# Turning attention values token-major with VectorE's 32x32 block transposes and stores of 128-byte pieces, in place of TensorE transposes and copies

## The chip, the core and the metric

The kernel runs on one core of a Trainium2 chip. The engines are TensorE (PE in the profile; its weight loads are a row of their own, PEld), VectorE (DVE), ScalarE (ACT), GpSimd (POOL) and SyncE (SP), which only issues DMAs. DMAs are issued here from SP's queue (hardware) and from GpSimd's (software). The metric is the device time of one execution, in microseconds (us), as the median of the runs shown.

## The reference: what is computed

A residual stream of 1024 tokens by 1024 features passes through two layers: a gated short convolution, and an attention over dilated windows. Only the second is touched. Cut to what matters:

```python
h = rms_norm(x, attn_norm)
proj = h @ w_in                       # per dilation group g of 3: q, k, v (1024 columns each); then z
for g, (window, dilation) in enumerate(((128, 1), (512, 4), (2048, 16))):
    q, k = rms_norm(q_g, q_gain[g]), rms_norm(k_g, k_gain[g])
    # query t attends to keys t - dilation*j: the sequence is split into `dilation`
    # residue classes, each evaluated in banded blocks of 128 queries
    logits = q @ k.T * HEAD_DIM ** -0.5 + bias          # 16 heads of 64
    out_g, lse_g = softmax(logits) @ v_g, logsumexp(logits)
o = sum over g of softmax_over_g(lse_g) * out_g
x = x + (o * silu(z)) @ w_out
```

## The kernel before, in words

The program runs in four stages, of which the third is the one that is edited: (1) the convolution's input projections, 0 to some 620 us; (2) its output projection, up to some 862 us; (3) the projections of the attention layer, to some 1622 us, here called the projection stage; (4) the attention itself with its output projection, to the end.

Data lie with features on the 128 partitions and tokens along the free axis. Matrix products are made in float32r: each operand is split into a high part (`ACTIVATE ws<-...`, line 164, on ScalarE) and a low part (`TENSOR_TENSOR ws<-...`, line 165, on VectorE), and three products (lines 301, 303, 304) make one.

In the projection stage two blocks of 128 output columns are taken together, as a *pair*, by seven Strassen-like products of 12 matmuls each. `pairs` (line 598) lists 40 of them: two pairs of kind "qk" (each the q and k of one *unit*, a unit being a head pair `hp` and a dilation group `g`), then one of kind "v" (the values of the same two units), twelve times over, with four pairs of kind "z" between and behind. TensorE takes the products of pair n in the order 1, 2, 4 of the pair before, 6, 5, 3 of the pair before, 7. In the profile a product is known by its right-hand operand: 1 `blke`, 2 `blkf`, 4 `blka`, 6 `xb`, 5 `blkd`, 3 `blkb`, 7 `blkg`. Products 1, 6, 7 and 4 of one pair add up in one PSUM bank `v["x"]`. After 1, 6 and 7 ScalarE copies the bank's state out (`copied`, line 309), and the next product of the bank can begin when that copy is done; after 4, the finished result is taken. VectorE adds these copies to the other bank (`added`, line 313). A result goes to `got`: for "qk" it is squared and summed; for "v" it is multiplied by the tokens' norm factors `R1` into a spare SBUF area (`blkc` in the profile, line 682), on VectorE when it comes from PSUM and on GpSimd otherwise.

Weights are loaded by SP (`wr`, line 159), mixed by GpSimd (`sr`, line 276) and split into eight rotating buffers `ws`. While pair n is multiplied, one split of pair n + 1 follows each product.

The attention needs V token-major: tokens on partitions, the two heads' 128 features along the free axis. `turn(col, q)` does that for half the tokens of one unit: four TensorE transposes against `ident` into one PSUM bank (line 729), one copy to an SBUF tile `f` (VectorE for q = 1, line 732; ScalarE for q = 0, line 734) and one store of 256 KB to the DRAM tile `vd` from GpSimd's queue (line 735). The four turns of a "v" pair n stand behind the products 2, 4, 6 and 5 of pair n + 2. That pair has no `norm`, the work on q and k which stands in the pairs two behind each "qk" pair. In stage (4) `load_v` (line 839) fetches a unit's V with two DMAs of 128 partitions from SP's queue, two steps before the unit's first step.

The order on TensorE is the order of the code in stages (1) to (3) (`manual_schedule`); the other engines' order there is set by a scheduler from its own estimates. In stage (4) all engines keep the order of the code. Each engine works strictly in its order. Completions of DMAs from SP (and from ScalarE, had it any) are counted on eight semaphores, `DMAHW0` to `DMAHW7`, which the framework hands out in turn; a DMA that reuses one waits until the previous DMA on it has landed.

Of the kernel before, what the change touches and what calls it, by code (L numbers as in the profile page):

```python
# [10 lines left out]
F32 = mybir.dt.float32  # L11
F32R = mybir.dt.float32r
I32 = mybir.dt.int32
AF = mybir.ActivationFunctionType
OP = mybir.AluOpType
# [4 lines left out]
P = 128  # L20
D = 1024
S = 1024
KT = D // P
HALF = 512
# [4 lines left out]
HP = H // 2  # L29
G = 3  # L30
# [5 lines left out]
def trunk(ctx: ExitStack, tc: tile.TileContext, a, out):  # L36
    nc = tc.nc
    consts = ctx.enter_context(tc.tile_pool(name="consts", bufs=1))
    dram = ctx.enter_context(tc.tile_pool(name="dram", bufs=1, space=DRAM))
# [32 lines left out]
    ident = const("ident", [P, P])  # L72
# [43 lines left out]
    sk1 = dram.tile([H, P * 385], F32, name="sk1")  # L116
    sk2 = dram.tile([H, P * 257], F32, name="sk2")
    qkd = dram.tile([HP, G, 2, P, S], F32, name="qkd")
    vd = dram.tile([HP, G, 2, P, HALF], F32, name="vd")
    zd = dram.tile([HP, P, S], F32, name="zd")  # L120
    nld = dram.tile([HP, 2, S * 4], F32, name="nld")
    fd = dram.tile([HP, G, 2, S], F32, name="fd")
# [1 line left out]

    def half(hf):
        return slice(hf * HALF, hf * HALF + HALF)

    def blk(t, g, b):
        if g == 0:
            return t[:, b * P:(b + 1) * P]  # L130
        if g == 1:
            return t.rearrange("p (n s c) -> p c n s", n=2, c=4)[:, b // 2, b % 2]
        return t[:, b * P:(b + 1) * P]

    with tc.tile_pool(name="wq", bufs=1) as wq, tc.tile_pool(name="sle", bufs=1) as sle, \
            tc.tile_pool(name="sl", bufs=1) as sl, \
# [370 lines left out]
        with tc.tile_pool(name="ev", bufs=1, side="right", reuse_waits="tile") as ev, tc.tile_pool(name="xb", bufs=1, side="right", reuse_waits="tile") as xb, \  # L507
# [122 lines left out]
            units = [(hp, g) for hp in range(HP) for g in range(G)]  # L630
# [16 lines left out]
            def spare():  # L647
                if not space:
                    space["t"] = block("c").rearrange("p a b c -> p (a b c)").bitcast(F32)
                return space["t"]  # L650
# [6 lines left out]
            def pair(n, w):  # L657
                p = pairs[n]
# [3 lines left out]
                def got(col, hf, t, ps=None):  # L662
                    cs = half(hf)
                    if kind == "qk":
                        if ps is not None:
                            t = copied(ps)
                        u[col, hf] = t
                        if "st" not in u:
                            u["st"] = sm.tile([P, 2, 32], F32, name="st", tag="st")
                        sq = ftile()  # L670
                        nc.scalar.activation(sq, t, AF.Square)  # L671
                        nc.vector.tensor_reduce(out=u["st"][:, col, hf * 16:(hf + 1) * 16],
                                                in_=sq.rearrange("p (c q) -> p c q", q=32), op=OP.add, axis=AX.X,
                                                apply_transpose=True)
                    elif kind == "v":
                        vt = spare()[:, col * S + hf * HALF:col * S + hf * HALF + HALF]
                        eng, t, r = (nc.vector, ps, R1[:, cs]) if ps is not None else (nc.gpsimd, t, R1[:, cs])
                        if units[p[1] + col][1] == 2:
                            vt = spare()[:, col * S:col * S + S].rearrange("p (r x i) -> p i x r", r=4, x=4)
                            vt = vt[:, hf * 32:hf * 32 + 32]  # L680
                            t, r = (y.rearrange("p (i x r) -> p i x r", x=4, r=4) for y in (t, r))
                        eng.tensor_tensor(vt, t, r, op=OP.mult)  # L682
                    else:
                        if ps is not None:
                            t = ftile()
                            nc.vector.tensor_tensor(t, ps, R1[:, cs], op=OP.mult)
                        else:
                            nc.gpsimd.tensor_tensor(t, t, R1[:, cs], op=OP.mult)
                        nc.scalar.activation(t, t, AF.Silu)
                        nc.gpsimd.dma_start(zd[p[1] + col, :, cs], t)  # L690
# [29 lines left out]

                def turn(col, q):
                    hp, g = units[p[1] + col]
                    vt = spare()[:, col * S:col * S + S]
                    if q:
                        pv = cps.tile([P, 4, P], F32, name="pp", tag="pp")
                    else:
                        pv = cst.tile([P, 4, P], F32, name="st", tag="st")
                    for i in range(4):
                        nc.tensor.transpose(pv[:, i], blk(vt, g, 4 * q + i), ident)
                    o = ftile()  # L730
                    if q:
                        nc.vector.tensor_copy(o, pv.rearrange("p a b -> p (a b)"))
                    else:
                        nc.scalar.activation(o, pv.rearrange("p a b -> p (a b)"), AF.Copy)
                    nc.gpsimd.dma_start(vd[hp, g, q], o)

                if kind == "qk":
                    due[n + 2, 0] = [norm]
# [76 lines left out]
    with tc.tile_pool(name="sp", bufs=1, space=PSUM) as sp, tc.tile_pool(name="ptp", bufs=2, space=PSUM) as ptp, \  # L815
# [11 lines left out]
        QK, VS, SZ, y2, part, ml = {}, {}, {}, {}, {}, {}  # L827
# [10 lines left out]

        def load_v(hp, g):
            VS[hp, g] = ap.tile([P, 8, P], F32, name="V", tag="V", bufs=3)  # L840
            for q in range(2):
                nc.sync.dma_start(VS[hp, g][:, 4 * q:4 * q + 4].rearrange("p a b -> p (a b)"), vd[hp, g, q])


        banks = [sp.tile([P, 4, P], F32, name="ps", tag=f"ps{i}") for i in range(3)]
# [337 lines left out]
        for un in units:  # L1183
            st, prefetch = attention(*un)
# [16 lines left out]
        for r in range(3):  # L1201
            k0 = at[2 * r + 2, 0][0] + LD
            k = k0
            for i, (dt, hf) in enumerate(tiles):
                late = k >= len(steps)
                name = "pd"
# [125 lines left out]
```

## Time and profile before

| what | value |
|---|---|
| runs | 1952.8, 1958.64, 1959.34 us; median 1958.64 |
| span of the profiled execution | 1952.1 us |
| its time outside the span | not recorded apart; the span is 0.7 us below the lowest run |
| busy share of PE, PEld, DVE, ACT, POOL | 98%, 79%, 77%, 45%, 44% |
| projection stage | 862 to 1622 us |
| stores of `vd` | 48, 256 KB each |

The profile is taken from one execution. A row of a group gives its line, engine, operation, tiles written and read, and the durations of one instruction as minimum, median and maximum in ns. A row of a timeline gives start, duration, engine, line, operation. A row of the waits gives who waited for whom, us in total, times, the longest. Matmuls overlap, so their durations say less than the distance of their starts.

### The profile page before, as it was taken

The page shows a single profiled execution, that of the slowest core. Times are in us where ns is not written, and L with a number is a line of the kernel's source. Part 1 is how long each engine was busy: PE and PEld are TensorE (multiplying, and loading weights), DVE is VectorE, ACT ScalarE, POOL GpSimd, SP SyncE. Part 2 cuts the span into 40 slices and gives each one's busy share as a digit, 9 for nine tenths or more (in the row PEclk, how much of TensorE's full clock was granted, in tenths as well). Part 3 has the DMA queues.
Part 4 walks back from the last instruction along what each step waited for, and adds up shares of the span by engine and source line. Part 5 has one row for each costly group of instructions (what it writes and reads, how often), then busy time and mean ns, then how long its engine had stood idle before and what let it go on. Part 6 is the DMA issues. An engine that isn't in the chain of part 4 may idle for free.

```text
span 1952.1 us, 30599 instructions
## 1 busy us (share of the span) xinstructions
PE 1906.1 (98%) x10894; PEld 1549.5 (79%) x10894; DVE 1495.5 (77%) x2769; ACT 886.4 (45%) x2031; POOL 850.0 (44%) x775
## 2 busy tenths in 40 slices
PE   8999999999999999999999999999999999889999
PEld 6888888888888888888878888878888886667777
DVE  7866766666665655698898689869888886889996
ACT  6433333333333444453433433444343437877780
POOL 0366666676665211433444443444344442433330
PEclk9999999999999999999999999999999999999999
DMA  6312232323223665432323232232232336887852
GB/s 200 117 58 89 87 94 85 101 72 103 79 84 109 215 208 189 138 103 87 129 87 124 92 111 101 103 108 97 87 129 87 127 110 243 253 278 230 250 149 87
DMA packets 117033, 253.79 MB, mean 130 GB/s; under 512 B 17726, under 2 KB 23070, under 8 KB 116880
## 3 DMA queue, kind: packets, MB, share of 16 engines
q1 hardware_dynamic: 93280, 176.89, 28.0%
q0 software_dynamic: 23600, 74.95, 11.4%
q8 instruction: 85, 1.39, 0.3%
q14 instruction: 68, 0.56, 0.1%
HBM read 192.53 MB, written 67.64 MB: 133 GB/s over the span
## 4 chain that ended last, share of the span: by engine, by line
PE 77%; DVE 11%; issue 4%; DMA 4%; ACT 2%; POOL 1%; SPq 0%; DVEq 0%; POOLq 0%; ACTq 0%
PE pp L301 18%; PE pp L304 18%; PE pp L303 18%; PE pp L552 3%; PE pp L553 3%; PE pp L551 3%; DVE ws L165 2%; DVE blkc L716 2%; PE pt L949 2%; PE po L970 1%; PE pp L374 1%; PE pp L376 1%; PE pp L375 1%; ACT xs L942 1%; DVE ri L67 1%
## 5 line engine op out<-in xcount | busy, mean ns | idle before, releaser
L165 DVE TENSOR_TENSOR ws<-wr,ws 128x512 fp32r<-128x512 f32 x284 | 273.1, 963 | 120.3 <-ACT ws L164 119.2
L164 ACT ACTIVATE ws<-wr 128x512 fp32r<-128x512 f32 x284 | 178.3, 629 | 355.0 <-PE pp L304 232.3
L164 ACT ACTIVATE ws<-sr 128x512 fp32r<-128x512 f32 x272 | 169.9, 629 | 294.1 <-PE pp L304 235.1
L276 POOL TENSOR_TENSOR sr<-wr 128x512 f32<-128x512 f32 x136 | 186.7, 1373 | 260.8 <-DMA wr<-in_conv_w_in 68.1
L165 DVE TENSOR_TENSOR ws<-sr,ws 128x512 fp32r<-128x512 f32 x272 | 226.6, 841 | 77.8 <-ACT ws L164 75.6
L313 DVE TENSOR_TENSOR f<-pp,f 128x512 f32<-128x512 f32 x204 | 139.5, 684 | 87.3 <-PE pp L304 80.6
L942 ACT ACTIVATE xs<-xs,nl 128x256 f32<-128x256 f32 (+2 forms) x384 | 160.4, 423 | 0.0
L309 ACT ACTIVATE f<-pp 128x512 f32<-128x512 f32 x228 | 132.5, 581 | 24.6 <-POOL blkc L682 11.0
L671 ACT ACTIVATE f<-f 128x512 f32<-128x512 f32 x96 | 60.7, 632 | 138.4 <-DVE f L313 100.9
L276 POOL TENSOR_TENSOR sr<-wr,sr 128x512 f32<-128x512 f32 x68 | 88.4, 1301 | 71.3 <-issue 46.8
L301 PE MATMUL pp<-blkg,ws 128*128 128x512 f32 x272 | 107.3, 394 | 4.6 <-ACT f L309 4.6
L936 DVE CUSTOM_DVE_ANT_0 xs<-ps,bt 128x256 f32<-128x256 f32 (+2 forms) x384 | 102.3, 324 | 10.1 <-ACT xs L942 4.2
L301 PE MATMUL pp<-blkf,ws 128*128 128x512 f32 x272 | 108.6, 399 | 0.7 <-ACT f L309 0.7
L301 PE MATMUL pp<-blka,ws 128*128 128x512 f32 x272 | 107.3, 394 | 1.5 <-ACT f L309 1.5
L301 PE MATMUL pp<-blkb,ws 128*128 128x512 f32 x272 | 107.3, 395 | 0.0
L276 POOL TENSOR_TENSOR sr<-sr,wr 128x512 f32<-128x512 f32 x68 | 104.9, 1543 | 4.9
L301 PE MATMUL pp<-blkd,ws 128*128 128x512 f32 x272 | 107.0, 393 | 0.0
L304 PE MATMUL pp<-blkf,ws 128*128 128x512 f32 x272 | 106.3, 391 | 0.0
L304 PE MATMUL pp<-blkd,ws 128*128 128x512 f32 x272 | 106.0, 390 | 0.0
L304 PE MATMUL pp<-blka,ws 128*128 128x512 f32 x272 | 106.0, 390 | 0.0
L304 PE MATMUL pp<-blkb,ws 128*128 128x512 f32 x272 | 106.0, 390 | 0.0
L303 PE MATMUL pp<-blkg,ws 128*128 128x512 f32 x272 | 105.9, 389 | 0.0
(341 smaller groups left out, 5271.7 us busy)
## 6 DMA issues: line engine op xcount, KB each, us to landing
wr<-in_conv_w_in SPq DMA_DIRECT2D x128, 256.0 KB, 3.1
wr<-in_wqk SPq DMA_DIRECT2D x96, 256.0 KB, 3.0
qkd<-blkc POOLq DMA_DIRECT2D x48, 512.0 KB, 3.4
qk<-qkd SPq DMA_DIRECT2D x48, 512.0 KB, 5.2
wr<-in_conv_w_out SPq DMA_DIRECT2D x64, 256.0 KB, 3.2
f<-in_x SPq DMA_DIRECT2D x48, 256.0 KB, 4.4
wr<-in_wv SPq DMA_DIRECT2D x48, 256.0 KB, 3.2
vd<-f POOLq DMA_DIRECT2D x48, 256.0 KB, 2.6
```

The source lines that it names most:

```text
L164: nc.scalar.activation(t[:, 0], src, AF.Copy)
L165: nc.vector.tensor_tensor(t[:, 1], src, t[:, 0].bitcast(F32), op=OP.subtract)
L276: nc.gpsimd.tensor_tensor(t, x, y, op=op)
L301: nc.tensor.matmul(ps, w[:, 0, ws], b[:, k, 0], start=new and k == 0, stop=False, skip_group_check=not new)
L303: nc.tensor.matmul(ps, w[:, 0, ws], b[:, k, 1], start=False, stop=False, skip_group_check=not new)
L304: nc.tensor.matmul(ps, w[:, 1, ws], b[:, k, 0], start=False, stop=end and k == 3, skip_group_check=not new)
L309: nc.scalar.activation(t, ps, AF.Copy)
L313: nc.vector.tensor_tensor(m, ps, m, op=OP.add)
L551: nc.tensor.matmul(ps[dt], w[:, 0, ws], b[:, k, 0], start=(q == k == 0), stop=False)
L671: nc.scalar.activation(sq, t, AF.Square)
L936: nc.vector.tensor_tensor_reduce(out=x, in0=flat[s][:, cols], in1=u["bt"][s][:, bs], op0=OP.add, op1=OP.min, scale=-1.0, scalar=3e38, accu ...
L942: nc.scalar.activation(x, x, AF.Exp, bias=nm, scale=-1.0, accum_out=L)
```

## The change

`turn` no longer uses TensorE or PSUM. The multiplication in `got` writes V into the spare area in an order in which a 32x32 block transpose of VectorE (each block of 32 partitions by 32 elements turned by itself) leaves, on partition 32a + q, tokens q and features 32a to 32a + 31 as runs of 32 floats. Four DMAs from ScalarE's queue store the tile, one for each block of 32 partitions, each as 32 x 16 pieces of 128 bytes, to a `vd` that has another shape. `load_v` fetches it by four DMAs of 32 partitions, 4 KB per partition. For the third dilation group the multiplication is made in two halves.

```diff
-    vd = dram.tile([HP, G, 2, P, HALF], F32, name="vd")
+    vd = dram.tile([HP, G, 32, 32, P], F32, name="vd")
...
                     elif kind == "v":
-                        vt = spare()[:, col * S + hf * HALF:col * S + hf * HALF + HALF]
+                        vt = spare()[:, col * S:col * S + S]
                         eng, t, r = (nc.vector, ps, R1[:, cs]) if ps is not None else (nc.gpsimd, t, R1[:, cs])
-                        if units[p[1] + col][1] == 2:
-                            vt = spare()[:, col * S:col * S + S].rearrange("p (r x i) -> p i x r", r=4, x=4)
-                            vt = vt[:, hf * 32:hf * 32 + 32]
-                            t, r = (y.rearrange("p (i x r) -> p i x r", x=4, r=4) for y in (t, r))
-                        eng.tensor_tensor(vt, t, r, op=OP.mult)
+                        g = units[p[1] + col][1]
+                        if g == 0:
+                            vt = vt.rearrange("p (x n b q) -> p n b x q", x=4, n=2, b=4)[:, hf]
+                            t, r = (y.rearrange("p (b x q) -> p b x q", b=4, x=4) for y in (t, r))
+                        elif g == 1:
+                            vt = vt.rearrange("p (x c n q) -> p n c x q", x=4, c=4, n=2)[:, hf]
+                            t, r = (y.rearrange("p (x q c) -> p c x q", x=4, c=4) for y in (t, r))
+                        if g == 2:
+                            vt = vt.rearrange("p (x n c h q) -> p n h x c q", x=2, n=2, c=4, h=2)[:, hf]
+                            t, r = (y.rearrange("p (q h x c) -> p h x c q", h=2, x=2, c=4) for y in (t, r))
+                            for h in range(2):
+                                eng.tensor_tensor(vt[:, h], t[:, h], r[:, h], op=OP.mult)
+                        else:
+                            eng.tensor_tensor(vt, t, r, op=OP.mult)
...
                 def turn(col, q):
                     hp, g = units[p[1] + col]
-                    vt = spare()[:, col * S:col * S + S]
-                    if q:
-                        pv = cps.tile([P, 4, P], F32, name="pp", tag="pp")
-                    else:
-                        pv = cst.tile([P, 4, P], F32, name="st", tag="st")
-                    for i in range(4):
-                        nc.tensor.transpose(pv[:, i], blk(vt, g, 4 * q + i), ident)
+                    vt = spare()[:, col * S + q * HALF:col * S + q * HALF + HALF]
                     o = ftile()
-                    if q:
-                        nc.vector.tensor_copy(o, pv.rearrange("p a b -> p (a b)"))
-                    else:
-                        nc.scalar.activation(o, pv.rearrange("p a b -> p (a b)"), AF.Copy)
-                    nc.gpsimd.dma_start(vd[hp, g, q], o)
+                    nc.vector.transpose(o.rearrange("p (c q) -> p c q", q=32), vt.rearrange("p (c q) -> p c q", q=32))
+                    to = vd[hp, g].rearrange("q c (a d) -> a q c d", d=32)[:, :, 16 * q:16 * q + 16]
+                    for a in range(4):
+                        nc.scalar.dma_start(to[a], o[32 * a:32 * a + 32].rearrange("q (c d) -> q c d", d=32))
...
         def load_v(hp, g):
             VS[hp, g] = ap.tile([P, 8, P], F32, name="V", tag="V", bufs=3)
-            for q in range(2):
-                nc.sync.dma_start(VS[hp, g][:, 4 * q:4 * q + 4].rearrange("p a b -> p (a b)"), vd[hp, g, q])
+            for x in range(4):
+                nc.sync.dma_start(VS[hp, g][32 * x:32 * x + 32], vd[hp, g, :, 8 * x:8 * x + 8])
```

What it moves is seen in the first pair with `turn`. On TensorE, between products 2 and 4, there stood before:

```order
L304 MATMUL pp<-blkf,ws 128x512
L729 MATMUL st<-ident,blkc 128x128 x4
L301 MATMUL pp<-blka,ws 128x512
L303 MATMUL pp<-blka,ws 128x512
L304 MATMUL pp<-blka,ws 128x512
```

Now the first matmul on `blka` follows the last on `blkf`; so it does at all 48 places.

On ScalarE the same pair ran as follows before (the first row is the square behind a "qk" result, the row of L734 the copy of the first turn):

```order
L671 ACTIVATE f<-f 128x512
L734 ACTIVATE f<-st 128x512
L164 ACTIVATE ws<-wr 128x512
L309 ACTIVATE f<-pp 128x512
L671 ACTIVATE f<-f 128x512
L164 ACTIVATE ws<-sr 128x512
L309 ACTIVATE f<-pp 128x512
L734 ACTIVATE f<-st 128x512
L164 ACTIVATE ws<-sr 128x512 x2
L671 ACTIVATE f<-f 128x512
L164 ACTIVATE ws<-wr 128x512
L309 ACTIVATE f<-pp 128x512
```

and runs as follows now (line numbers of the changed kernel: 157 for 164, 302 for 309, 664 for 671):

```order
L664 ACTIVATE f<-f 128x512
L730 DMA vd<-f 32x16x32 x4
L157 ACTIVATE ws<-wr 128x512
L302 ACTIVATE f<-pp 128x512
L664 ACTIVATE f<-f 128x512
L157 ACTIVATE ws<-sr 128x512
L302 ACTIVATE f<-pp 128x512
L730 DMA vd<-f 32x16x32 x8
L157 ACTIVATE ws<-sr 128x512
L730 DMA vd<-f 32x16x32 x4
L157 ACTIVATE ws<-sr 128x512
L664 ACTIVATE f<-f 128x512
```

Behind the last row follow, as before, one split and the copy of `v["x"]` after product 7. The second and third turn's stores stand together behind the copy after product 6, and the fourth's behind one split more. With what they wait for, the second to the fourth turn's stores read:

```order
L730 DMA vd<-f 32x16x32 [waits DVE_49]
L730 DMA vd<-f 32x16x32
L730 DMA vd<-f 32x16x32 [waits DMAHW4_49]
L730 DMA vd<-f 32x16x32 [waits DMAHW5_49]
L730 DMA vd<-f 32x16x32 [waits DMAHW6_49,DVE_49]
L730 DMA vd<-f 32x16x32 [waits DMAHW7_49]
L730 DMA vd<-f 32x16x32 [waits DMAHW0_49]
L730 DMA vd<-f 32x16x32 [waits DMAHW1_49]
L157 ACTIVATE ws<-sr 128x512 [waits PE_49]
L730 DMA vd<-f 32x16x32 [waits DMAHW2_49,DVE_49]
L730 DMA vd<-f 32x16x32 [waits DMAHW3_49]
L730 DMA vd<-f 32x16x32 [waits DMAHW4_49]
```

`DVE_49` is VectorE's block transpose. Semaphores 4 and 5 were last used by a load of weights, 6, 7, 0 and 1 by the first turn's stores, and those of the fourth turn's stores (2 to 5) by the second turn's.

VectorE's part of the same place, before:

```order
L165 TENSOR_TENSOR ws<-wr,ws 128x512
L672 TENSOR_REDUCE st<-f 128x16
L165 TENSOR_TENSOR ws<-wr,ws 128x512
L732 COPY f<-pp 128x512
L672 TENSOR_REDUCE st<-f 128x16
```

and now:

```order
L158 TENSOR_TENSOR ws<-wr,ws 128x512
L727 STREAM_TRANSPOSE f<-blkc 128x512
L665 TENSOR_REDUCE st<-f 128x16
L158 TENSOR_TENSOR ws<-wr,ws 128x512
L727 STREAM_TRANSPOSE f<-blkc 128x512 x3
L665 TENSOR_REDUCE st<-f 128x16
```

The first block transpose stands one split earlier than the first copy did, and the other three together where it stood.

More of the change, by code (lines that the diff above doesn't have):

```diff
@@ L126, in half @@
         return slice(hf * HALF, hf * HALF + HALF)
[L128 to L133, printed above, removed]
     with tc.tile_pool(name="wq", bufs=1) as wq, tc.tile_pool(name="sle", bufs=1) as sle, \
```

## The prediction

> **What bounds the kernel now.** I read the page first (busy shares, chain), then the busy time by stage, then the stage in which the change lies, in order of time.
>
> ```profile
> PE 1906.1 (98%) x10894; PEld 1549.5 (79%) x10894; DVE 1495.5 (77%) x2769; ACT 886.4 (45%) x2031; POOL 850.0 (44%) x775
> PE 77%; DVE 11%; issue 4%; DMA 4%; ACT 2%; POOL 1%; SPq 0%; DVEq 0%; POOLq 0%; ACTq 0%
> 862.00:1622.00 760.00, 750.40 (x3390) 615.25 (x3389) 632.57 (x944) 298.70 (x520) 323.17 (x300) 1.00 0.31 108
> 1622.00:1800.00 178.00, 160.11 (x2210) 120.52 (x2209) 154.98 (x662) 143.96 (x582) 58.90 (x74) 0.96 0.82 256
> PE pp L301 <- ACT f L309: 6.0, 13, 1.3
> PEld pp L301 <- ACT f L309: 11.9, 14, 1.8
> PE st L694 <- DVE st L672: 2.8, 8, 0.4
> PE st L729 <- POOL blkc L682: 0.8, 1, 0.8
> ACT ws L164 <- PE pp L304: 243.5, 167, 2.7
> ```
>
> The third and fourth rows are stages: length, then busy time of PE, weight loads, DVE, ACT and POOL, granted clock, DMA share, GB/s. The removed transposes lie in the projection stage, 862 to 1622: TensorE is busy 750.4 of 760.0 us at full clock, the DMA engines 31%. The next four rows are TensorE's waits there: for the copies of L309 under 2 us each, for VectorE and GpSimd 3.6 us in all. The last says that ScalarE, with the splits of the weights, waits for TensorE to free their buffers: it is ahead. A microsecond taken from TensorE's row of instructions is therefore worth a microsecond, until another engine makes TensorE wait. What an instruction of that row costs has to be read from starts, since matmuls overlap:
>
> ```profile
> 1165.72 0.39 PE L303 MATMUL pp<-blkd,ws 128*128 128x512 f32 x1
> 1165.95 0.39 PE L304 MATMUL pp<-blkd,ws 128*128 128x512 f32 x1
> 1166.18 0.60 PE L729 MATMUL pp<-ident,blkc 128*128 128x128 f32 x4
> 1166.53 0.48 PE L301 MATMUL pp<-blkb,ws 128*128 128x512 f32 x1
> 1166.85 0.39 PE L303 MATMUL pp<-blkb,ws 128*128 128x512 f32 x1
> ```
>
> Products start every 0.227 us (1165.72 to 1165.95, rounded). From 1165.95 to 1166.85 are 0.90 us for two steps, which alone take 0.453: four transposes cost 0.447 us.
>
> **The change, part by part.**
>
> ```profile
> L729 PE MATMUL st<-ident,blkc x96: 270/272/385, 894.0 to 1609.8; 128*128 128x128 f32 x96
> L729 PE MATMUL pp<-ident,blkc x96: 270/272/286, 897.1 to 1613.0; 128*128 128x128 f32 x96
> L732 DVE COPY f<-pp x24: 676/687/693, 900.0 to 1613.3; 128x512 f32<-128x512 f32 x24
> L734 ACT ACTIVATE f<-st x24: 577/586/594, 897.3 to 1610.2; 128x512 f32<-128x512 f32 x24
> L735 POOL DMA_DIRECT2D vd<-f x48: 540/540/600, 902.4 to 1614.3; - x48
> L704 DVE STREAM_TRANSPOSE f<-ri x96: 667/669/714, 861.0 to 1592.1; 128x512 f32<-128x512 f32 x96
> L682 DVE TENSOR_TENSOR blkc<-pp,sqacc x12: 645/652/1055, 883.0 to 1592.7; 128x512 f32<-128x512 f32 x12
> L682 POOL TENSOR_TENSOR blkc<-f,sqacc x36: 1278/1304/1792, 858.6 to 1600.7; 128x512 f32<-128x512 f32 x36
> ```
>
> 1. TensorE loses 192 transposes, 48 groups of four: 48 x 0.447 = 21.5 us, all on the path.
>
> 2. VectorE loses 24 copies of 0.687 and gets 48 block transposes, which the row of L704 prices at 0.669: 32.1 - 16.5 = +15.6 us over the stage, in which it is busy 632.6 of 760. All of it falls in the 12 pairs that hold `turn`, which have no `norm`. I take 0; what hides it is that pair's idle time on VectorE. ScalarE loses 24 x 0.586 = 14.1 us, GpSimd 48 x 0.54 = 25.9 us of issuing.
>
> 3. The multiplications of V write another order. For the second dilation group the reads become strided (4 instructions on VectorE, 12 on GpSimd); the third already was, and is the maximum of both L682 rows: from 0.652 up to 1.055 and from 1.304 up to 1.792, so 4 x 0.40 + 12 x 0.49 = 7.5 us at most, and 0 at least. For the third group each becomes two halves, a fixed cost more. Only where a copy of L309 waits for a tile that GpSimd still reads does it reach TensorE: I take 2 us.
>
> 4. The stores are the open term. 48 of 256 KB on GpSimd's queue become 192 of 64 KB on ScalarE's, each 512 pieces of 128 bytes. ScalarE issues in order, so whatever an issue costs, and whatever it waits for, delays the copies, squares and weight splits behind it. I call the price of one issue c. No DMA is issued from ScalarE now. The nearest rows:
>
> ```profile
> L879 SPq DMA_DIRECT2D bt<-sk x32: 319/320/1221, 1603.2 to 1854.0; - x32
> L877 SPq DMA_DIRECT2D bt<-sk x32: 444/546/1485, 1623.3 to 1862.6; - x32
> L990 POOL DMA_DIRECT2D nld<-nl x8: 902/908/927, 1638.1 to 1881.1; - x8
> L992 POOL DMA_DIRECT2D nld<-nl x8: 727/732/740, 1646.9 to 1895.4; - x8
> ```
>
> L879 moves 128 pieces of 1 KB on SP's hardware queue in 0.32, L877 64 pieces of 256 bytes in 0.55. GpSimd's queue, whose price grows with the pieces, takes 0.73 for 256 (L992) and 0.91 for 1024 (L990), so some 0.78 for 512. The ends are 0.32 and 0.91. I take 0.55: L877 is nearest in kind (a hardware queue, small pieces, part of the partitions), and L879 against it shows no growth with the count of pieces. What TensorE can bear is read from the first pair with `turn`:
>
> ```profile
> 893.96 0.60 PE L729 MATMUL st<-ident,blkc 128*128 128x128 f32 x4
> 896.65 0.68 DVE L165 TENSOR_TENSOR ws<-wr,ws 128x512 fp32r<-128x512 f32 x1
> 897.77 0.62 ACT L164 ACTIVATE ws<-wr 128x512 fp32r<-128x512 f32 x1
> 898.30 0.59 ACT L309 ACTIVATE f<-pp 128x512 f32<-128x512 f32 x1
> 910.25 0.58 ACT L309 ACTIVATE f<-pp 128x512 f32<-128x512 f32 x1
> 915.22 0.39 PE L301 MATMUL pp<-blka,ws 128*128 128x512 f32 x1
> ```
>
> In the new order VectorE makes the first block transpose behind the split of 896.65, done near 898.0. Then ScalarE issues 4 stores (4c), runs five instructions at one start per 0.53 us (897.77 to 898.30; 2.7 us), issues 8, runs one, issues 4, runs three and then the copy that stood at 910.25 (12c, and 2.7 us for the five). So that copy ends at 898.0 + 5.4 + 16c = 903.4 + 16c. TensorE needs it, since the product on `blka` adds to the bank that it reads: 915.22 before, and 4 x 0.447 earlier once the four groups from 893.96 on are gone, 913.4. The slack is 10.0 - 16c: 1.2 us at c = 0.55, none at c = 0.625; beyond it each of the 12 pairs costs 16c - 10.0. The splits of weights are delayed too, but each takes the one of eight buffers that a product has just left, and is used six products or more later: 6 x 12 x 0.227 = 16 us. At c = 0.55 I take 0.
>
> 5. The program counts hardware DMAs on eight semaphores that SP and ScalarE share; the last four stores of a pair wait until the second four have landed. Issue to issue between these lie 8c + 0.5 = 4.9 us, and 1.2 of slack: landings up to 6.1 us cost nothing.
>
> ```profile
> vd<-f POOLq DMA_DIRECT2D x48, 256.0 KB, 2.6
> nld<-nl POOLq DMA_DIRECT2D x1, 16.0 KB, 2.0
> DMA to landing us min/median/max: 1.8/5.8/10.5
> ```
>
> The second row is the store of L992 at 1895, 256 pieces of 64 bytes with the DMA engines idle: 2.0 us. The third holds all transfers through `nld`, in a stage with the DMA engines 82% busy. The stage of the change has 31%, so I take about 3 us, hidden. [...]
>
> 6. V is loaded by 4 transfers of 32 partitions in place of 2, 48 issues more on SP:
>
> ```profile
> 1627.02 1.89 SPq L842 DMA_DIRECT2D V<-vd  x2
> 1640.04 1.09 PE L970 MATMUL po<-pts,V 128*64 128x128 f32 x16
> SPq L877 <- DMA bt<-sk: 8.7, 4, 3.5
> ```
>
> This load, the tightest that I found, is issued 13 us before its first use, so 2 x 0.4 us of issues more are hidden. SP already waits there for earlier landings (third row), and doubling may stretch that; 0 to 3 us, I take 0.
>
> The sum: 1952.1 - 21.5 + 2 = 1932.6 for the profiled span. That span is 0.7 below the lowest of the three runs and 6.5 below their median, 1958.64; on the median the forecast is 1958.64 - 19.5 = 1939.1.
>
> **The rivals.**
>
> Rival 1, slower: the issue price. If 512 pieces cost ScalarE what GpSimd's rows say, c = 0.78 to 0.91, the `blka` product waits 2.5 to 4.6 us for the copy of L309 in each of 12 pairs, 30 to 55 us: 1969 to 1994. It cancels the gain at 16c - 10.0 = 19.5 / 12, c = 0.73. For it: the pieces are four times any hardware DMA's here, in three dimensions, and L877 is dearer than L879. Against it: L877 moves half the pieces.
>
> Rival 2, slower: the pieces land late. With landings of 10.5 us, the maximum above, 10.5 - 6.1 = 4.4 us by 12 pairs are 53 us: 1992. Against it: the 2.0 us, and idle DMA engines.
>
> Rival 3, no change: VectorE and GpSimd take it back. If all 7.5 us of part 3 and the 15.6 us of part 2 came to TensorE, -21.5 + 23.1 gives 1960. Against it: the 3.6 us in the first fence, and GpSimd is relieved of 25.9.
>
> In between lies c from 0.63 to 0.76, where TensorE gives part or all of it back: 1940 to 1965.
>
> **How the numbers follow.** The forecast case has 0.52 and its own range is 1930 (nothing given back, the 0.8 us wait of L729 gone too, counted from the lowest run) to 1945 (all of part 3, from the highest). In between 0.16, of which 0.06 faster, 0.08 the same, 0.02 slower; rival 1 0.20; rival 2 0.07; rival 3 0.05, of which 0.03 the same and 0.02 slower. About 0.3% (5.9 us) is what a measurement of this kernel can tell from no change. Faster 0.58, the same 0.11, slower 0.31. Left out of the range are the upper part of rivals 1 and 2 (c over about 0.85, some 0.15) and 0.04 below: 1929 to 1985.
>
> **What would show it.** No `ident` rows in TensorE's projection stage, and that stage about 20 us shorter than 760 with TensorE still busy all but some 10 us of it. Issues of `vd` on ScalarE's queue of about 0.55 us; at 0.75 or more, waits of TensorE for L309's successor grow from 18 us to 50 and the gain is gone. Landings of `vd` near 3 us; over 6, rival 2. Waits of ScalarE for VectorE's transposes, which I took as none beyond 898.0, would make it wrong without either price. The attention stage should keep its 330 us.

## The result, and the profile after

The change made the kernel slower: 1981.99 us as the median of four runs (1972.99 to 1988.04) against 1958.99 of the kernel before, timed beside it (1952.8 to 1960.16); the ratio is 1.0125, 95% interval 1.0104 to 1.0147. The profiled execution took 1978.78 us, its span 1977.0.

First the busy shares, the chain of work that ended last, and two stretches, the projection stage as it was bounded before and the first part of the attention (length; busy time of PE, PEld, DVE, ACT, POOL; granted clock, DMA share, GB/s):

```profile
PE 1895.1 (96%) x10702; PEld 1534.5 (78%) x10702; DVE 1517.5 (77%) x2797; ACT 868.6 (44%) x2007; POOL 844.4 (43%) x739
PE 60%; DVE 23%; issue 5%; DMA 5%; ACT 4%; ACTq 3%; SPq 0%; POOL 0%; DVEq 0%; POOLq 0%
862.00:1622.00 760.00, 723.14 (x3145) 588.30 (x3144) 653.46 (x966) 277.16 (x490) 312.92 (x257) 0.99 0.35 102
1622.00:1800.00 178.00, 151.99 (x1929) 114.60 (x1928) 134.85 (x579) 129.41 (x508) 57.94 (x76) 0.94 0.93 249
```

The 192 transposes are gone (10894 matmuls to 10702). But TensorE, which was busy 750.4 of the 760 us, is now busy 723.1, at a clock of 0.99, and the chain runs through VectorE for 23% of the span instead of 11%. The loads of V mark the end of the projection stage, before and after:

```profile
L842 SPq DMA_DIRECT2D V<-vd x48: 319/382/1444, 1622.5 to 1873.8; - x48
...
L837 SPq DMA_DIRECT2D V<-vd x96: 302/413/1327, 1640.7 to 1899.5; - x96
```

The first load is issued 18.2 us later than before, where it should have come some 20 us earlier; from there to the end it is 336.3 us (1977.0 - 1640.7) where it was 329.6. So about 40 us were lost in the projection stage and, by this one pair of profiles, 7 in the attention. The waits in the projection stage (us in total, times, longest), and the rows of the new instructions:

```profile
PE pp L294 <- ACT f L302: 27.3, 18, 2.7
PE st L696 <- DVE st L665: 9.5, 11, 1.8
...
L730 ACTq DMA_DIRECT2D vd<-f x192: 309/515/1656, 899.6 to 1632.3; - x192
vd<-f ACTq DMA_DIRECT2D x192, 64.0 KB, 2.0
L727 DVE STREAM_TRANSPOSE f<-blkc x48: 660/685/708, 898.8 to 1624.9; 128x512 f32<-128x512 f32 x48
```

TensorE waits 36.8 us for a copy of ScalarE or for the sums of squares, instead of 8.8 in the same two rows before. Yet an issue takes the 0.515 us that was forecast, a landing 2.0 us, a block transpose 0.685. How the loss comes about is seen in the first pair with `turn` and the one behind it. The kernel before, in order of time (start, duration, engine, line):

```profile
905.78 1.30 POOL L276 TENSOR_TENSOR sr<-wr,sr 128x512 f32<-128x512 f32 x1
907.11 4.79 SPq L159 DMA_DIRECT2D wr<-in_wqk  x4
914.38 1.29 POOL L276 TENSOR_TENSOR sr<-wr 128x512 f32<-128x512 f32 x1 [7.30 <-DVE rit L65]
918.24 1.30 POOL L682 TENSOR_TENSOR blkc<-f,sqacc 128x512 f32<-128x512 f32 x1
920.77 0.23 DVE L67 SCALAR_TENSOR_TENSOR ri<-rit,ri 128x64 f32<-128x64 f32 x1
925.25 0.63 ACT L671 ACTIVATE f<-f 128x512 f32<-128x512 f32 x1 [3.70 <-DVE blkc L716]
925.79 0.58 ACT L309 ACTIVATE f<-pp 128x512 f32<-128x512 f32 x1
926.42 0.50 PE L301 MATMUL pp<-blkg,ws 128*128 128x512 f32 x1 [0.16 <-ACT f L309]
```

and the changed kernel:

```profile
904.49 4.19 ACTq L730 DMA_DIRECT2D vd<-f  x8
908.72 0.63 ACT L157 ACTIVATE ws<-sr 128x512 fp32r<-128x512 f32 x1 [4.26 <-PE pp L297]
910.21 1.28 POOL L269 TENSOR_TENSOR sr<-wr,sr 128x512 f32<-128x512 f32 x1 [6.93 <-issue]
911.52 2.87 SPq L152 DMA_DIRECT2D wr<-in_wqk  x4
911.55 0.61 ACT L664 ACTIVATE f<-f 128x512 f32<-128x512 f32 x1
913.04 0.43 PE L696 MATMUL st<-st,swap 128*128 128x64 f32 x2 [1.69 <-DVE st L665]
917.80 1.29 POOL L269 TENSOR_TENSOR sr<-wr 128x512 f32<-128x512 f32 x1 [6.31 <-DMA wr<-in_wqk]
922.12 2.20 POOL L682 TENSOR_TENSOR blkc<-f,sqacc 128x256 f32<-128x256 f32 x2
923.35 1.06 DVE L67 SCALAR_TENSOR_TENSOR ri<-rit,ri 128x64 f32<-128x64 f32 x1
924.36 0.60 ACT L302 ACTIVATE f<-pp 128x512 f32<-128x512 f32 x1 [4.66 <-POOL blkc L682]
927.42 3.89 DVE L718 SCALAR_TENSOR_TENSOR blkc<-f,gain 128x512 f32<-128x512 f32 x4
928.59 0.63 ACT L664 ACTIVATE f<-f 128x512 f32<-128x512 f32 x1 [3.12 <-DVE blkc L718]
929.13 0.58 ACT L302 ACTIVATE f<-pp 128x512 f32<-128x512 f32 x1
929.76 0.55 PE L294 MATMUL pp<-blkg,ws 128*128 128x512 f32 x1 [2.58 <-ACT f L302]
```

Eight issues hold ScalarE for 4.19 us. The "wait for PE" of 4.26 us in the second row is that time: a queue that is issuing counts as idle. Behind the burst the split of a mixed weight comes late, so GpSimd's last mix of that weight (910.21, was 905.78), so the weight load that needs its buffer (911.52, was 907.11), so the next mixes (917.80, was 914.38). A multiplication of V stands behind these mixes and is itself longer, 2.20 us against 1.30. One copy of ScalarE waits for it 4.66 us (924.36), but it ends 4.8 us before TensorE goes on, which waits for the next one.

The way to TensorE goes through VectorE, which the profile's chain names as well. On the way the square of 911.55 comes late for the `swap` matmul of `norm`, which waits 1.69 us, and what `norm` then does on VectorE starts late. It also takes longer: its small instructions (L65 to L67, 128x64) take 0.2 us while GpSimd stands still and 1.0 to 1.3 us beside a GpSimd instruction. Before, the last four of them, up to the one of 920.77, stood behind GpSimd's work; now five, up to the one of 923.35, run beside it. The four multiplications by the gain (L718) start at 927.42 instead of 924.01; a square on ScalarE, which needs one of the rotating tiles `f` that they read, waits for the first of them (928.59, was 925.25); the copy behind the square (929.13, was 925.79) is the one that TensorE needs: 2.58 us lost instead of 0.16.

Three things could thus have cost the time: ScalarE's queue (Q), the longer multiplications on GpSimd (M), and, in the attention, the four loads of V (A).

### The profile page after: what moved, and what is told of

Its sections match the earlier page's. It is cut to its first block, busy times and chain, and to the rows that moved or that the text cites. A ratio compares the mean times of both kernels' runs of the same rounds, so it can differ in the third digit from the quotient of the medians.

```text
span 1977.0 us, 30537 instructions
## 1 busy us (share of the span) xinstructions
PE 1895.1 (96%) x10702; PEld 1534.5 (78%) x10702; DVE 1517.5 (77%) x2797; ACT 868.6 (44%) x2007; POOL 844.4 (43%) x739
## 4 chain that ended last, share of the span: by engine, by line
PE 60%; DVE 23%; issue 5%; DMA 5%; ACT 4%; ACTq 3%; SPq 0%; POOL 0%; DVEq 0%; POOLq 0%
PE pp L294 13%; PE pp L296 13%; PE pp L297 13%; DVE ws L158 6%; PE pp L545 3%; PE pp L546 3%; PE pp L544 3%; DVE blkc L718 3%; ACTq L730 3%; DVE rit L66 2%; ACT xs L937 2%; DMA nld<-nl 2%; DVE f L306 2%; DVE st L665 2%; DVE ri L67 2%
## 5 line engine op out<-in xcount | busy, mean ns | idle before, releaser
L158 DVE TENSOR_TENSOR ws<-sr,ws 128x512 fp32r<-128x512 f32 x272 | 230.9, 857 | 94.4 <-ACT ws L157 92.5
L294 PE MATMUL pp<-blkg,ws 128*128 128x512 f32 x272 | 109.0, 401 | 22.0 <-ACT f L302 22.0
L294 PE MATMUL pp<-blkf,ws 128*128 128x512 f32 x272 | 109.1, 401 | 0.7 <-ACT f L302 0.7
L296 PE MATMUL pp<-blkg,ws 128*128 128x512 f32 x272 | 107.9, 397 | 0.0
L297 PE MATMUL pp<-blkg,ws 128*128 128x512 f32 x272 | 107.7, 396 | 0.0
L297 PE MATMUL pp<-blkf,ws 128*128 128x512 f32 x272 | 106.9, 393 | 0.0
L296 PE MATMUL pp<-blkf,ws 128*128 128x512 f32 x272 | 106.6, 392 | 0.0
L294 PE MATMUL pp<-blkb,ws 128*128 128x512 f32 x272 | 106.2, 390 | 0.0
L294 PE MATMUL pp<-blke,ws 128*128 128x512 f32 x272 | 105.9, 389 | 0.0
L296 PE MATMUL pp<-blke,ws 128*128 128x512 f32 x272 | 105.9, 389 | 0.0
```

Source lines behind the costliest of these rows:

```text
L158: nc.vector.tensor_tensor(t[:, 1], src, t[:, 0].bitcast(F32), op=OP.subtract)
L294: nc.tensor.matmul(ps, w[:, 0, ws], b[:, k, 0], start=new and k == 0, stop=False, skip_group_check=not new)
L296: nc.tensor.matmul(ps, w[:, 0, ws], b[:, k, 1], start=False, stop=False, skip_group_check=not new)
L297: nc.tensor.matmul(ps, w[:, 1, ws], b[:, k, 0], start=False, stop=end and k == 3, skip_group_check=not new)
```

## The experiments

Each was timed beside runs of the kernel before on the same chip; runs of different rows are compared by their ratios.

| run | time, us | before, us | ratio, 95% interval |
|---|---|---|---|
| the change | 1981.99 | 1958.99 | 1.0125 (1.0104 to 1.0147) |
| e1_plain_mult | 1966.42 | 1954.91 | 1.0054 (1.0036 to 1.0073) |
| e2_sp_stores | 1966.84 | 1954.91 | 1.0053 (1.0035 to 1.0071) |
| e3_one_store | 1943.97 | 1954.91 | 0.9935 (0.9912 to 0.9959) |
| e4_one_store_plain | 1931.46 | 1954.91 | 0.9875 (0.9846 to 0.9904) |
| e5_read_in_order | 1965.06 | 1955.83 | 1.0048 (1.0027 to 1.0069) |
| e6_before_four_loads | 1965.94 | 1955.83 | 1.0051 (1.0034 to 1.0068) |
| e7_read_sp | 1947.05 | 1955.83 | 0.9962 (0.9940 to 0.9984) |
| e8_read_sp_one_load | 2025.31 | 1955.83 | 1.0344 (1.0306 to 1.0383) |
| e9_all_three | 1936.74 | 1957.38 | 0.9896 (0.9879 to 0.9913) |
| e10_all_but_queue | 1965.31 | 1957.38 | 1.0042 (1.0027 to 1.0058) |
| e11_before_four_wide | 1955.67 | 1957.38 | 0.9986 (0.9974 to 0.9998) |
| e12_all_three_one_load | 1938.84 | 1957.38 | 0.9906 (0.9888 to 0.9923) |
| e13_half_from_sp | 1934.23 | 1956.43 | 0.9906 (0.9887 to 0.9924) |
| e14_short_issues | 1953.64 | 1956.43 | 0.9994 (0.9980 to 1.0009) |

### One suspect at a time, and nearly all at once

```diff
 e1: eng.tensor_tensor(spare()[:, col * S + hf * HALF:col * S + hf * HALF + HALF], t, r, op=OP.mult)   # all groups
 e2: -nc.scalar.dma_start(to[a], ...)   +nc.sync.dma_start(to[a], ...)
 e3: +nc.scalar.dma_start(vd[hp, g, q], o)      # vd and load_v as before the change
 e4: e1, with +nc.gpsimd.dma_start(vd[hp, g, q], o)   # vd and load_v as before the change
```

> The changed kernel with V's multiplications written in plain token order again (512 contiguous columns in and out for all three groups, none in two halves); the stores and loads stay, so the tokens of V land in another order. Theory M (GpSimd's strided multiplications, 2.2 to 3.1 us for groups 1 and 2 where they were 1.3, keep the buffers that ScalarE's copies wait for): TensorE's gaps at the start of products, 32 us, shrink to the 8 us of before, and the time falls from 1982 to 1950-1960 us. Theory Q (the 192 issues on ScalarE delay everything behind them): the multiplications cost at most 5 us of the loss, and the time stays at 1974-1984 us.

> The changed kernel with its 192 stores issued by SyncE instead of ScalarE, nothing else. Theory Q: ScalarE gets back 99 us of issues and some 60 us of waits for earlier stores; TensorE's gaps in the projection stage fall from 42 us to about 15, and the time is 1945-1958 us. Theory M: the gaps stay, 1970-1985 us. A third way: SyncE's weight loads now stand behind the stores, which wait for VectorE's transposes, and come late, 1975-1995 us.

> The changed kernel with one contiguous 64 KB store for each turn (still from ScalarE, 48 issues instead of 192) and the two contiguous loads of before; block transposes and strided multiplications stay, so V's 32x32 blocks do not come together as rows. Theory Q: ScalarE loses 144 of 192 issues, 1950-1962 us. Theory M: 1970-1985 us. Theory A (the loss in the attention stage, 336 us instead of 330, comes from V's four loads of 32 partitions): its length goes back to 330 us, otherwise it stays at 336.

> Both at once: plain multiplications, and one contiguous 64 KB store for each turn, issued by GpSimd as before the change, with two contiguous loads. Only the block transposes in place of TensorE's transposes and the copies are left of the change (V's tokens are out of order). If M and Q together are the whole loss, TensorE's 21.5 us come out: 1934-1944 us. If something else is behind it (the transposes on VectorE themselves, which come when the scheduler likes and no longer when TensorE does), it stays above 1955 us.

Neither M nor Q alone was right: e1 and e2 each give back 0.7% (14 us) of the 1.25% and land between the two expectations. e3 fell below all of them, since it takes away most of Q and the four loads as well; its attention from the first load on, 1946.3 - 1612.2 = 334 us, lies between the two lengths that were to decide on A, and decides nothing. e4 shows that the core of the change is sound: block transposes on VectorE, with plain multiplications and V's tokens left out of order, are worth 23.5 us (1954.91 - 1931.46), about TensorE's 21.5. The 48 transposes on VectorE are hidden, as forecast. e3, which still has M and 48 stores on ScalarE, is 12.5 us above e4.

### What in the multiplications costs

```diff
-vt = vt.rearrange("p (x c n q) -> p n c x q", ...)[:, hf];  t, r: "p (x q c) -> p c x q"
+vt = vt.rearrange("p (x c n q) -> p n x q c", ...)[:, hf];  t, r: "p (x q c) -> p x q c"
-vt = vt.rearrange("p (x n c h q) -> p n h x c q", ...);     t, r: "p (q h x c) -> p h x c q"
+vt = vt.rearrange("p (x n c h q) -> p n h q x c", ...);     t, r: "p (q h x c) -> p h q x c"
```

> The changed kernel with another order of the same elements inside the strided multiplications: they now read the buffer and the row R1 in memory order and scatter what they write, where the change read at strides of 4 and 16 elements and wrote runs of 32. Same tokens, same places. Theory M, in the form that the strided READS cost GpSimd its time: the multiplications of groups 1 and 2 fall from 2.15-3.15 us to about 1.3-1.8 (before the change group 2 read in order and scattered its writes, at most 1.79 us), and the time is near that of the plain multiplications, 1962-1970 us. If scattered writes cost as much, nothing changes: 1975-1984 us.

The rows on GpSimd (minimum, median, maximum), first of the changed kernel, then of e5:

```profile
L684 POOL TENSOR_TENSOR blkc<-f,sqacc x24: 1285/1971/2601, 859.2 to 1616.8; 128x512 f32<-128x512 f32 x24
L682 POOL TENSOR_TENSOR blkc<-f,sqacc x24: 1103/1142/1708, 922.1 to 1597.6; 128x256 f32<-128x256 f32 x24
...
L684 POOL TENSOR_TENSOR blkc<-f,sqacc x24: 1280/1300/1791, 858.6 to 1602.8; 128x512 f32<-128x512 f32 x24
L682 POOL TENSOR_TENSOR blkc<-f,sqacc x24: 728/956/1288, 919.5 to 1584.8; 128x256 f32<-128x256 f32 x24
```

The first row of each holds the first two groups, the second row the halves of the third. The same elements, read in memory order and scattered on the way out, take 1.30 us instead of a median of 1.97 (group 0, read contiguously in both, is in this row too; group 1 alone took 2.14 to 2.60 in the changed kernel) and 0.96 per half instead of 1.14. e5 is as fast as e1, so the strided reads are the whole of M, and scattered writes on GpSimd cost nothing to see: 0.77% or 15 us. On VectorE, which makes a quarter of the multiplications, the medians are the same either way: 0.83 us with strided reads and 0.85 with scattered writes in the first two groups, 0.56 and 0.60 per half. So the gain is GpSimd's. The strided reads step 16 bytes in group 1 and 64 in group 2, and by the shortest times they take 1.7 times as long in group 1 (2.14 us, where the shortest of e5's row is 1.28) and 1.5 times per half (1.10 for 0.73). Why its reads at a step cost GpSimd this, and its writes do not, is not shown.

### The four loads

```diff
 e6, e11 (from the kernel before):
-for q in range(2): nc.sync.dma_start(VS[hp, g][:, 4 * q:4 * q + 4]..., vd[hp, g, q])
+e6:  for x in range(4): nc.sync.dma_start(VS[hp, g][32 * x:32 * x + 32]..., vd[hp, g]...[32 * x:32 * x + 32])
+e11: for q in range(4): nc.sync.dma_start(VS[hp, g][:, 2 * q:2 * q + 2]..., vd[hp, g, q // 2, :, q % 2 * 256:q % 2 * 256 + 256])
```

> The kernel before, with V loaded for each unit by four transfers of 32 partitions in place of two of 128; nothing else. Theory A: the attention stage grows from 327 to 333-337 us and the time is 1960-1966 us. If the four loads cost nothing by themselves (the loss of the attention stage comes from what the projection stage leaves late), it stays at 1953-1957 us.

> The kernel before, with V loaded by four transfers of 128 partitions x 256 columns in place of two of 512 columns. It parts theory A: if the number of transfers is what costs (four issues, four of the shared semaphores), 1962-1968 us as with four of 32 partitions; if it is that each transfer goes to 32 partitions alone, 1953-1958 us.

The first crowded stretch of the attention (columns as above), and the landings (KB each, median us), of the kernel before, e6 and e11:

```profile
1660.00:1740.00 80.00, 66.72 (x949) 50.53 (x946) 69.00 (x296) 64.40 (x260) 32.56 (x43) 0.91 0.84 254
V<-vd SPq DMA_DIRECT2D x48, 256.0 KB, 5.5
...
1660.00:1740.00 80.00, 63.78 (x863) 47.66 (x863) 62.27 (x273) 58.94 (x237) 28.63 (x36) 0.84 0.84 224
V<-vd SPq DMA_DIRECT2D x96, 128.0 KB, 6.5
...
1660.00:1740.00 80.00, 68.25 (x938) 51.97 (x940) 71.23 (x292) 64.81 (x263) 32.73 (x43) 0.89 0.85 254
V<-vd SPq DMA_DIRECT2D x96, 128.0 KB, 5.3
```

Four transfers of 32 partitions cost the kernel before 10 us; four of 128 partitions cost nothing. So it is not the number of issues or semaphores. Over all profiles, the stretch from the first load of V to the end is 336.3 to 344.9 us in the six runs with four loads of 32 partitions (mean 341.8) and 329.6 to 336.7 in the ten others (332.7): 9 us, but one pair alone can mislead. With the DMA engines busy to the same share, 224 GB/s move instead of 254, and half the bytes land 1.0 us later. Why a transfer to 32 partitions is the slower one is not shown.

### Do the costs add, and can all three be avoided?

```diff
 e7: e5 and e2 together
 e8: e7, with vd[hp, g] as [128 tokens, 8, 128]:
+for a in range(4):
+    for x in range(2):
+        nc.sync.dma_start(to[a, 2 * q + x], o[32 * a:32 * a + 32, 256 * x:256 * x + 256]...)   # 8 x 32 KB
+nc.sync.dma_start(VS[hp, g], vd[hp, g])
```

> The edit of the run named e5_read_in_order together with SyncE issuing the 192 stores. If the costs of the multiplications and of ScalarE's queue add up (13 and 13 us below the changed kernel), 1950-1957 us; if the one hides the other, 1960-1967 us.

> As e7_read_sp, but the tokens are put together by the store: eight stores of 32 KB for each turn (384 issues, on SyncE) and one contiguous load of 512 KB for each unit. Theory A with the sum of the others: 8 to 12 us below e7, so 1938-1947 us, and the attention stage is back at 327-331 us. Otherwise: SyncE's 384 issues (some 0.3-0.5 us each, up to 190 us of the 760) hold the weight loads up, and the time is above 1955 us.

e7 is 18.0 us under e5 and 18 under e2 by the ratios (0.0091): each of the two costs is at least as dear without the other as with it (14 to 15). So e7 fell below the 1950 that adding them gave, and the kernel with both mended is faster than the one before. e8 was the trap that its last sentence names, and worse:

```profile
L731 SPq DMA_DIRECT2D vd<-f x384: 549/607/1931, 901.3 to 1685.7; - x192
ACT ws L157 <- DMA wr<-in_wqk: 84.5, 14, 11.8
PE pp L294 <- ACT f L302: 68.5, 13, 7.3
```

384 issues at 0.607 us are 233 us on SyncE, and the weight loads queue behind them. Its attention, 336.7 us from the first load on, did not go back to the 327 to 331 expected either. The way out is another order of columns (the diff shows the patterns alone). If the partition that a token gets is 4q + x instead of 32x + q (for group 2: 64x + 2q + y), DRAM holds a unit as 128 complete rows with the same four stores:

```diff
 e9:
+g == 0: vt "p (x n b q) -> p n b q x"[:, hf];      t, r "p (b q x) -> p b q x"
+g == 1: vt "p (x c n q) -> p n q x c"[:, hf];      t, r "p (q x c) -> p q x c"
+g == 2: vt "p (x k c n u) -> p n x u k c"[:, hf];  t, r "p (u k x c) -> p x u k c"    # two halves, by x
+to = vd[hp, g].rearrange("(n q c a d) -> n a q c d" if g == 2 else "(q n c a d) -> n a q c d", ...)[q]
+for a in range(4): nc.sync.dma_start(to[a], o[32 * a:32 * a + 32]...)
+for q in range(2): nc.sync.dma_start(VS[hp, g][:, 4 * q:4 * q + 4]..., vd[hp, g].rearrange("(p n f) -> n p f", p=P, n=2)[q])
 (group 2 then finds its blocks of V at (vb + a) % 2 * 4 + (vb + a) // 2)
 e10: e9 with nc.scalar for the stores;   e12: e9 with one load of 512 KB
```

> Same result as the reference's, with all three suspected costs taken out: V's columns are ordered so that the block transposes bring a unit together in DRAM as 128 rows (token 4q+x for groups 0 and 1, 64x+2q+y for group 2), which two transfers of 128 partitions load as before the change; the multiplications read in memory order; SyncE issues the 192 stores. If the three costs add up (ScalarE's queue 13-18 us, strided reads 14-20, four loads of 32 partitions 10), it is 10 us below e7_read_sp: 1935-1941 us, against 1955 of the kernel before. If the four loads hurt only where the projection stage ends late: 1944-1950 us.

> As e9_all_three, but ScalarE issues the 192 stores, as the change does: theory Q by itself. Q: 13 to 18 us above e9, 1950-1958 us, about the time of the kernel before, with gaps of TensorE in the projection stage of 25 us instead of 10. If ScalarE's issues cost only while the strided reads hold its buffers up: within 5 us of e9.

> As e9_all_three, with V's two loads made one of 512 KB, as the loads of q and k are. If fewer transfers leave the queue freer, 2 to 5 us below e9; if the single landing comes later than the first of two (5.5 us for 256 KB, 5.2 to 6 for the 512 KB of q and k), up to 3 us above; most likely within 2 us of it.

e9 is faster than the kernel before by 1.04% (0.87 to 1.21), 20.6 us: TensorE's 21.5 us come out. e12 does the same. e10 is a surprise: with the other costs gone, ScalarE's queue alone costs 28.6 us, not 13 to 18. Most of it is seen in TensorE's row: its two waits of the projection stage, 28.7 us in e10 (shown below) and 10.0 in e9, and 44 matmuls (2 in e9) up to 1600 us that start some 0.42 us apart instead of 0.227, some 8 us more; the granted clock of 862 to 1622 us is 0.99 in e10 and 1.00 in e9.

### What in ScalarE's queue costs

```diff
 e13: -nc.scalar.dma_start(to[a], ...)   +(nc.sync, nc.scalar)[a % 2].dma_start(to[a], ...)      # from e10
 e14: +nc.scalar.dma_start(vd[hp, g]...[q, 32 * a:32 * a + 32], o[32 * a:32 * a + 32])           # from e10, 2 KB rows
```

> As e10_all_but_queue, with two of each turn's four stores issued by SyncE and two by ScalarE: 96 issues stay on ScalarE, at the same places of its order, in bursts of 2, 4 and 2 instead of 4, 8 and 4. If each microsecond of issuing costs alike, half of the 28.6 us between e9 (1936.7) and e10 (1965.3) stay: 1949-1953 us. If there is slack that a short burst fits into (TensorE's own room before a late copy or sum of squares), nearly all goes: 1937-1944 us. If what costs is the waits for semaphores shared by both queues, little goes: 1958-1966 us.

> As e10_all_but_queue, with each store's 64 KB written to 32 contiguous rows of 2 KB instead of 512 pieces of 128 bytes (V's blocks are not put together); number, size, place in ScalarE's order and semaphores are the same. An issue should take about 0.31 us instead of 0.51 (the single store of e3, 128 pieces, took 0.326). If the time that ScalarE is held is the cause: 60 us of issues instead of 99, bursts of 2.5 us instead of 4.2, and 1942-1954 us. If the number is the cause: 1960-1967 us.

Issues on ScalarE and TensorE's two waits in the projection stage, of e10, e14 and e13 in this order:

```profile
L733 ACTq DMA_DIRECT2D vd<-f x192: 309/517/2094, 897.3 to 1625.1; - x192
PE st L696 <- DVE st L665: 15.8, 15, 2.7
PE pp L294 <- ACT f L302: 12.9, 10, 2.1
...
L729 ACTq DMA_DIRECT2D vd<-f x192: 308/438/1894, 898.1 to 1608.4; - x192
PE pp L294 <- ACT f L302: 18.1, 15, 2.1
PE st L696 <- DVE st L665: 4.2, 11, 0.7
...
L733 ACTq DMA_DIRECT2D vd<-f x96: 309/606/1751, 896.6 to 1589.2; - x96
PE pp L294 <- ACT f L302: 6.1, 11, 1.2
PE st L696 <- DVE st L665: 2.7, 8, 0.4
```

ScalarE is held some 99 us (192 x 0.517), 84 and 58 (96 x 0.606, with as many issued by SyncE beside them). Against e9, by the ratios, that costs 28.6, 19 and 2 us (the intervals of e13 and e9 overlap); by the medians 28.6, 16.9 and nothing. The time that ScalarE is held fits, above a threshold: per pair with `turn`, of which there are 12, 8.3, 7.0 and 4.8 us of issues cost 2.4, 1.4 to 1.6 and next to nothing. On a straight line through the first two the cost ends at 4.4 to 5.2 us, an estimate. The number of issues is not the cause by itself, since e14 has all 192. In e13 the stores keep their places and share the eight semaphores as before, with half of them on ScalarE; that nearly all of the cost went speaks against the semaphores. So does the profile of the change: in all but four of the bursts on ScalarE an issue takes 0.55 us or less on average, so little waiting for landings can be in them. e14 does not give the short issue that was expected (0.438, not 0.31), so it tells the size of the cost less sharply than planned.

## Why the prediction was wrong

Three terms of the sum were too small: in part 4 the stores' delay on ScalarE, put at 0, in part 3 the multiplications, put at 2 us, and in part 6 the loads, put at 0. That the measured 1982 lies within the forecast's 1929 to 1985 is luck: its upper part was there for dear issues and late landings, and neither came.

- **Part 1, TensorE: right.** The kernels with the other costs out gain 20.6 us (e9) and 23.5 us (e4) against 21.5.
- **Part 2, VectorE: right.** 0.685 us for 0.669, hidden: e4 has all 48 and gains in full.
- **Part 3, multiplications: the term was mis-sized, 2 us for 15.** The bound of 1.792 was read as the cost of the third group's strides. It is not: e1, whose multiplications are all contiguous, has the same 1.792 on GpSimd; and in the kernel before it belongs to the first two groups, whose 24 contiguous multiplications take 1.278 to 1.792, where the third group's twelve take 1.296 to 1.757. On GpSimd the third group read in order and scattered its writes; the change makes the second and third group read at strides, which no row before showed. They take up to 2.60 us, and the halves, noted as "a fixed cost more", twice 1.14. The path was too narrow as well: besides the copies that wait for GpSimd, VectorE's small instructions beside it take 1.2 us for 0.23. How the 15 us divide between these two paths stays open. Rival 3 named GpSimd and VectorE, at 7.5 us for the whole of part 3.
- **Part 4, the issue price: right, and the slack beside it wrong.** c is 0.515 (forecast 0.55), the copy ended at 913.2, where 903.4 + 16c puts it at 911.6, and the `blka` product, which began at about 916, did not wait for it. But the room was read from that one copy. Other rows of the same fences had none: the `swap` matmul of `norm` already waited for the sums of squares (L694, 8 times), whose square stands in the same queue; and the splits, dismissed as needed six products later, free the buffers of the weight loads and of GpSimd's mixes. The room per pair is some 4.4 to 5.2 us of issues (the estimate above), not 10.0, and the term is 14 to 29 us, not 0. So the loss that rival 1 described came at a price at which the forecast said it would not, and by other waits than that of the `blka` product.
- **Part 5, landings: right.** 2.0 us. Rival 2 did not come about. That the pieces are small shows in the landing by 0.3 us at most: the same 64 KB in rows of 2 KB land in 1.7 us (e14).
- **Part 6, loads: mis-sized, 0 for 10 us.** The forecast counted issues and semaphores, and both are free (e11: four transfers of 128 partitions, 1955.67 us for 1957.38). What costs is that each transfer goes to 32 partitions (e6: 1965.94 for 1955.83).

The sum made again with measured terms: -20.6 (e9) + 18.0 (Q, e5 to e7) + 15.1 (M, 0.77%, the change to e5) + 10.1 (A, e6) = +22.6 us; measured +23.0. It proves less than it seems to: e9, e7, e5 and the change follow each other by one edit at a time, so their differences must add up. Only A comes from elsewhere, and the step from e7 to e9 puts it at 12.9 us (0.66%). Q measured 14, 18 and 29 us in three settings.

## What to carry to other kernels

Before work is moved into an engine's in-order queue, look for the instruction behind it with the least room, along every chain that starts there (copies, statistics, and buffers that free loads), not only the nearest consumer. Work that grows on GpSimd can also come to stand beside VectorE's: here VectorE's small instructions took a median of 1.22 us beside it and at most 0.23 otherwise. When a layout change makes an access strided, ask for each engine whether the read or the write takes the stride: here the same multiplication on GpSimd took 2.14 to 2.60 us with the strides on the input (group 1) and a median of 1.30, that of the contiguous ones, with them on the output. In a stage with busy DMA engines, prefer transfers that span all 128 partitions (four of 32 cost 10 us here, four of 128 nothing); if a layout forces 32, look for another order of elements, which here cost nothing and brought 0.7% (e7 to e9).

## What the runs showed of the hardware that was not expected

Instructions of VectorE and of GpSimd take longer side by side. In the projection stage of the kernel before, 74 instructions of VectorE on 128x64 elements run for more than half of their time beside a GpSimd instruction on two tiles; their median is 1.22 us. Of the 146 that run beside none, none is over 0.23. The other way round, GpSimd's instructions of 128x512 that take 1.6 to 1.85 us instead of 1.3 run for more than a quarter of their time beside VectorE's low parts `ws<-wr,ws` in 40 of 45 cases, the short ones in 16 of 146. That it is the overlap was not tried by itself.

TensorE paid for some waits twice. Behind the wait of 929.76 the matmuls start every 0.42 us instead of every 0.227, for 3.4 us:

```profile
930.11 0.63 PE L296 MATMUL pp<-blkg,ws 128*128 128x512 f32 x1
930.53 0.63 PE L297 MATMUL pp<-blkg,ws 128*128 128x512 f32 x1
```

The granted clock of the 60 us from 922 is 0.97, where it was 1.00. It does not follow every wait: of the 18 waits over 0.8 us between 862 and 1600 us, four (1.85 to 2.75 us) are followed by such a stretch, and two of 2.53 and 2.55 us are not. In all it is 29 matmuls and some 6 us. What decides it is not shown. In the attention e6 has a lower clock too, 0.84 for 0.91.

Small pieces do cost the DMA engines, and the landing a little (2.0 us for 1.7). Queue, packets, MB and share of 16 engines' span, of the change (128-byte pieces), of e14 (2 KB rows, as many stores of 32 partitions) and of e3 (2 KB rows, 128 partitions):

```profile
q10 hardware_dynamic: 101376, 12.60, 4.2%
...
q10 hardware_dynamic: 9216, 12.60, 2.6%
...
q10 hardware_dynamic: 6912, 12.59, 1.7%
```

For the same 12.6 MB the pieces take 1.6 times the DMA engines' time of the rows, and four stores of 32 partitions 1.5 times that of one store of 128. The change's 4.2% of its 1977 us are 83 us; over the projection stage's 760 us that is 0.11, of the 0.35 that the DMA engines are busy there.
